# Key blocks of 114 keys instead of 128 in the attention of a decoder block

## The chip, the cores and the metric

The kernel runs on one core of a Trainium2 chip. The metric is the device time of one execution in microseconds (us), and less is better. The engines are named as in the profile: PE is TensorE's matmul and PEld its weight load, DVE is VectorE, ACT is ScalarE, POOL is GpSimd, SP is SyncE, which issues DMAs.

## The reference

One layer of a decoder: 16 learned tokens are put ahead of 1024 tokens of 1024 features (float32), then come a mixer and a gated MLP. The mixer runs a short convolution and an attention with 16 heads of 64 features side by side. Only the attention is touched here. It is a stick-breaking attention: no softmax, but a product of survival factors, taken from the query backwards.

```python
def stick_breaking_attention(q, k, v):
    # A[t,s] = sigmoid(z_ts) * prod_{s<j<t} (1 - sigmoid(z_tj)), s < t
    ...
        z = jnp.einsum("bqhd,bkhd->bhqk", qb, kb, ...) * scale
        causal = s_idx < t_idx
        log_beta = jax.nn.log_sigmoid(z)
        log_fail = jnp.where(causal, log_beta - z, 0.0)
        survive = lax.cumsum(log_fail, axis=3, reverse=True) - log_fail
        a = jnp.where(causal, jnp.exp(log_beta + survive), 0.0)
        o = jnp.einsum("bhqk,bkhd->bqhd", a, vb)
```

## The kernel before, in words

There are 1040 positions. The first 14 give no output, so 1026 queries remain: nine query blocks of `QB` = 114, in three groups `g` of three (`CH` = 342 queries). Query block `b` sees the keys from 0 to `nk` = 128 + 114 b, so the query blocks end at 128, 242, 356, 470, 584, 698, 812, 926 and 1040 keys.

Values that a product needs in more precision than one reduced-precision number gives are split into a high and a low part (`split`, lines 63 to 65: ACT copies the high part, DVE or POOL subtracts it). A dense product of the projections (`Dense.run`, lines 128 to 130, tile `mm`) is three matmuls for each block of 128 features: high by high, high by low, low by high.

Attention works through units of head pair `p`, head `h` and group `g`, in two stages that are Python generators:

- `stage1` computes the scores of a query block (`z`, lines 330 and 331), two sigmoids on ACT (`fl`, what survives, and `be`, the weight), the running product on DVE (a scan over `fl`, L340), and on POOL the weight `be` times the product (L346), a mask of the last 114 columns (`affine_select`, L348), and where the last key block that meets this query block reaches beyond `nk`, a memset of zeros up to its end (L353). `be` has queries on the partitions and keys in the columns.
- `stage2` goes over the key blocks `kb` of the group. For each it transposes the part of `be` of every query block that reaches the key block (L381, into the PSUM tile `tp`: keys on the partitions now), splits the result into `ah` and `al` (L64 on ACT, L65 on DVE), and two key blocks later multiplies: `av` += `vv[kb]` by `ah` (L371) and by `al` (L372). `vv` is the stationary operand, with the keys as contraction rows and 128 columns. A query block that doesn't reach a key block is left out on the left, so the moving operand has 342, 228 or 114 columns.

The values `vv` come from `item_v`: the features of v are transposed into blocks of keys by `tokens` (L262), nine blocks a head pair.

What sets the order of the work: the loop of lines 510 to 540 picks the next piece of `stage1` or `stage2` by the costs `COST1` and `COST2`, and after each piece puts in as many steps of the dense products (`dense.step`, three matmuls each) as the piece's share earns. So dense matmuls stand between most steps of attention on PE's queue. `stage2` yields `COST2[g] / (nkb + 3)` a piece, where `nkb` is its count of key blocks. The framework that builds the program adds the waits by the regions that instructions read and write, and has put some of the memsets ahead of work that stands before them in the code. `tp` has two PSUM buffers, `be` has six buffers and `fl` two.

Of the kernel before, what the change touches and what calls it, by code (L numbers as in the profile page):

```python
# [14 lines left out]
P = 128  # L15
# [7 lines left out]
QB = CH // 3  # L23
# [3 lines left out]
EPS = 1e-6  # L27
HALF = [(0, 258), (258, 256)]
NJ = 514


@with_exitstack
def block_kernel(ctx, tc, x, meta_tokens, g_pre_mix, w_in, channels, w_proj_conv,
                 w_proj_attn, w_out, g_post_mix, g_pre_ffn, w_up_gate, w_down,
                 g_post_ffn, out):
    nc = tc.nc

    def pool(name, bufs=1, side="left", space=None):
        kw = dict(name=name, bufs=bufs, reuse_waits="tile")
        if space is not None:  # L40
            kw["space"] = space
        else:
            kw["side"] = side
        return tc.tile_pool(**kw)
# [18 lines left out]
    def split(hi, lo, src, lo_engine=None):  # L63
        nc.scalar.copy(hi, src)  # L64
        (lo_engine or nc.vector).tensor_tensor(lo, src, hi.bitcast(F32), op=ALU.subtract)  # L65
# [93 lines left out]
    def col_block(w, c):  # L159
        return w[c]  # L160
# [84 lines left out]
    def item_v(p):  # L245
        st = {}

        def evac(ci, a, n, ps):
            if ci == 0:
                st["vt"] = work.tile([P, NT], F32, name="vt", tag="wk", bufs=4)  # L250
            vt = st["vt"]
            nc.scalar.copy(vt[:, a:a + n], ps)
            if ci < 2:
                return
            vv = heads.tile([P, 9, 2, P], F32R, name="vv", tag="vv", bufs=2)
            V[p] = vv

            def tokens(k0, kn, m):
                tp = ps_tp.tile([P, 512], F32, name="tp", tag="tp")
                for k in range(kn):  # L260
                    s0 = (k0 + k) * P
                    nc.tensor.transpose(tp[:m, k * P:(k + 1) * P], vt[:, s0:s0 + m], ident)  # L262
                tv = tp[:m, :kn * P].rearrange("p (k h d) -> p k h d", k=kn, h=2)
                split(vv[:m, k0:k0 + kn, :, 0:64], vv[:m, k0:k0 + kn, :, 64:128], tv)

            dense.defer(1, lambda: tokens(0, 4, P))
            dense.defer(2, lambda: tokens(4, 4, P))
            dense.defer(3, lambda: tokens(8, 1, 16))
        return (col_block(w_in, 40 + p), src_x, CH_K, evac)

    def items_conv(cb):
# [43 lines left out]
    def stage1(p, h, g):  # L315
        res = []
        qh, ql, kk = QH[p][h], QL[p][h], KK[p][h]
        nk_end = P + QB * (3 * g + 2)
        for b in range(3 * g, 3 * g + 3):
            nk = P + QB * b  # L320
            q0 = QB * b
            fl = work.tile([P, NT], F32, name="fl", tag="fl")[:QB]
            be = work.tile([P, NT], F32, name="be", tag="be", bufs=6)[:QB]
            nch = -(-nk // 512)
            wch = 2 * (-(-nk // (2 * nch)))
            c0 = 0
            while c0 < nk:
                n = min(wch, nk - c0)
                z = ps_z.tile([P, 512], F32, name="z", tag="z")[:QB, :n]
                nc.tensor.matmul(z, qh[:, q0:q0 + QB], kk[:, c0:c0 + n], start=True, stop=False)  # L330
                nc.tensor.matmul(z, ql[:, q0:q0 + QB], kk[:, c0:c0 + n], start=False, stop=True)  # L331
                nc.scalar.activation(fl[:, c0:c0 + n], z, AF.Sigmoid, scale=-0.125)  # L332
                nc.scalar.activation(be[:, c0:c0 + n], z, AF.Sigmoid, scale=0.125)
                c0 += n
                if late:
                    late.pop(0)()
                if c0 < nk:
                    yield n
            def weights(fl=fl, be=be, nk=nk):
                nc.vector.tensor_tensor_scan(fl[:, :nk][:, ::-1], fl[:, :nk][:, ::-1],  # L340
                                             upper[:, NT - nk:][:, ::-1], 1.0,
                                             op0=ALU.mult, op1=ALU.max)
                w = -(-(nk - 1) // (-(-nk // 384)))
                for a in range(0, nk - 1, w):
                    e = min(a + w, nk - 1)
                    nc.gpsimd.tensor_tensor(be[:, a:e], be[:, a:e], fl[:, a + 1:e + 1],  # L346
                                            op=ALU.mult)
                nc.gpsimd.affine_select(out=be[:, nk - QB:nk], in_=be[:, nk - QB:nk],  # L348
                                        pattern=[[-1, QB]], compare_op=ALU.is_gt, fill=0.0,
                                        base=0, channel_multiplier=1)  # L350
                pad = min(P * (-(-nk // P)), nk_end)
                if pad > nk:
                    nc.gpsimd.memset(be[:, nk:pad], 0.0)  # L353

            late.append(weights)
            res.append((be, nk))
            if len(res) == 3:
                units[(p, h, g)] = res
            yield n

    def stage2(p, h, g):
        blocks = units.pop((p, h, g))
        vv = V[p]
        nk_end = blocks[-1][1]
        nkb = -(-nk_end // P)
        av = ps_av.tile([P, 512], F32, name="av", tag="av")[:, :CH]
        pend = []

        def products(kb, n, off, ah, al):
            w = vv[:n, kb, h, :]  # L370
            nc.tensor.matmul(av[:, off:], w, ah[:n, off:], start=(kb == 0), stop=False)  # L371
            nc.tensor.matmul(av[:, off:], w, al[:n, off:], start=False, stop=(kb == nkb - 1))  # L372

        unit = COST2[g] / (nkb + 3)
        for kb in range(nkb):
            n = min(P, nk_end - kb * P)
            js = [j for j in range(3) if blocks[j][1] > kb * P]
            off = QB * js[0]
            tp = ps_tp.tile([P, 512], F32, name="tp", tag="tp")
            for j in js:  # L380
                nc.tensor.transpose(tp[:n, QB * j:QB * (j + 1)], blocks[j][0][:, kb * P:kb * P + n],  # L381
                                    ident[:QB, :QB])
            ah = work.tile([P, CH], F32R, name="ah", tag="ah", bufs=4)
            al = work.tile([P, CH], F32R, name="al", tag="al", bufs=4)
            split(ah[:n, off:], al[:n, off:], tp[:n, off:CH])
            pend.append((kb, n, off, ah, al))
            if len(pend) > 2:
                products(*pend.pop(0))
            yield unit
        while pend:  # L390
            products(*pend.pop(0))
            yield unit
        if (h, g) == (0, 0):
            OT[p] = work.tile([P, NT], F32, name="ot", tag="wk", bufs=4)
        ot = OT[p]
        a, b = (0, 64) if h == 0 else (64, 0)
        o = ot[a:a + 64, CH * g:CH * (g + 1)]
        nc.scalar.copy(o, av[b:b + 64])
        nc.vector.tensor_tensor(o, av[a:a + 64], o, op=ALU.add)
        if (h, g) == (1, 2):  # L400
            nc.sync.dma_start(o_d[p * P:(p + 1) * P, :], ot[:, :NQ])
        yield unit
# [17 lines left out]
    dense = Dense(ps_mm, items)  # L420
# [67 lines left out]
    def stream1():  # L488
        for u in units_in_order:
            for c in stage1(*u):  # L490
                yield c, u

    def stream2():
        for u in units_in_order:
            for c in stage2(*u):
                yield c, u
# [65 lines left out]
    k = 0  # L562
# [70 lines left out]
    k = 0  # L633
# [42 lines left out]
    early = x_ctx.enter_context(pool("early"))  # L676
    ops = {name: early.tile([P, 2, 4, NJ], F32R, name=f"op{name}") for name in ("B11", "T1")}
    par_ffn = early.tile([P, 66], F32, name="par_ffn")
# [95 lines left out]
    def op_split(name, r, which, engine):  # L774
        t = ops[name][:, :, :, r[0]:r[1]]
        split(t[:, 0], t[:, 1], quarter(r, which), engine)
# [18 lines left out]
    R0 = HALF[0]  # L795
    R1, R2 = (258, 399), (399, NJ)
    RL = (258, NJ)

# [171 lines left out]
    for b in range(9):  # L970
# [3 lines left out]
        for c in range(3):  # L974
            ps = out_products(b, c)
            if (b, c) == (8, 2):
# [4 lines left out]
                for name in ("T3", "B21", "T2"):  # L981
                    ops[name] = late.tile([P, 2, 4, NJ], F32R, name=f"op{name}")
                op_split("T2", R0, "O1", nc.vector)
# [19 lines left out]
    for k, _ in enumerate(products(0, *HALF[0], bank_of(ps_mm2, "mm"), evac_u(*HALF[0]))):  # L1003
        if k == 0:
            next(prep0)
        elif k == 1:
# [3 lines left out]
            for name in ("T4", "B22"):  # L1010
                ops[name] = late2.tile([P, 2, 4, NJ], F32R, name=f"op{name}")
        elif k == 2:
# [121 lines left out]
    for gi, fbs in enumerate(groups):  # L1134
# [14 lines left out]
        for tb in range(8):  # L1149
# [23 lines left out]
            if last:  # L1173
                a, hb, s0 = accs[tb], hbs[tb], ssqs[tb]
# [64 lines left out]
```

## Time and profile before

| | |
|---|---|
| time, median of three runs | 2033.37 us (2033.12, 2033.37, 2041.17) |
| span of the profiled execution | 2040.5 us |
| the run that the span fits | 2041.17 us, the only one longer than the span |
| PE busy | 1980.9 us, 97% of the span |
| DVE, ACT, POOL busy | 49%, 42%, 50% |
| stretch in which attention runs | about 60 to 990 us |
| mean granted clock of PE, whole span | 0.994 |

A row of a group of instructions gives line, engine and operation, output <- inputs, the shapes, the count, then busy time in us and the mean of one in ns, and behind the second bar the idle time of the engine just before them, with what ended it. In the rows of PE and PEld a shape such as `58*128 58x114` means contraction rows * columns of the stationary operand, and then the operand that is read, partitions x elements. A row of the timeline gives start and duration in us. A row of the waits says who waited for whom: total us, times, longest. A row of the stretches gives its length, the busy time of PE, PEld, DVE, ACT and POOL with their counts of instructions, the granted clock of PE, and the share and rate of DMA. Matmuls overlap, and their ends are modelled.

### The profile page before, as it was taken

How to read it: one execution, taken by the hardware profiler on the slowest of the kernel's cores; microseconds unless marked ns; L12 is line 12 of the kernel's file. 1: busy time of each engine (PE TensorE's matmuls, PEld its weight loads, DVE VectorE, ACT ScalarE, POOL GpSimd, SP SyncE). 2: the span in 40 equal slices, each digit the busy share in tenths (PEclk: the TensorE clock that was granted, in tenths of full speed). 3: DMA queues.
4: the chain of work that ended last, by engine and by line, in shares of the span. 5: the costliest groups of instructions: out<-in, count | busy, mean ns of one | idle time of the engine just before them, and what ended most of it. 6: DMA issues, size and time to landing. Idle time of an engine off the chain costs nothing.

```text
span 2040.5 us, 31024 instructions
## 1 busy us (share of the span) xinstructions
PE 1980.9 (97%) x12228; PEld 1857.9 (91%) x12228; DVE 1008.2 (49%) x1545; ACT 852.2 (42%) x1771; POOL 1025.7 (50%) x1142
## 2 busy tenths in 40 slices
PE   6999999999999999999999989979999999999997
PEld 6999999999999999999999989968998998878886
DVE  6445555555555555653331115784444434445547
ACT  5544554545454545554421213453344344421122
POOL 2644666565555646565223550246465655654353
PEclk9999999999999999999999999989999999999999
DMA  3111101111111111012574664312221212253223
GB/s 136 42 63 42 53 31 63 42 53 42 42 53 42 57 38 62 32 57 78 175 229 156 180 180 130 101 47 95 92 82 63 104 63 83 73 178 118 86 83 135
DMA packets 56175, 177.59 MB, mean 87 GB/s; under 512 B 12872, under 2 KB 12872, under 8 KB 56028
## 3 DMA queue, kind: packets, MB, share of 16 engines
q1 hardware_dynamic: 52704, 165.09, 24.7%
q10 hardware_dynamic: 3324, 10.50, 1.7%
q8 instruction: 96, 1.57, 0.3%
q14 instruction: 51, 0.42, 0.1%
HBM read 131.36 MB, written 44.21 MB: 86 GB/s over the span
## 4 chain that ended last, share of the span: by engine, by line
PE 82%; DVE 7%; DMA 5%; ACT 2%; POOL 2%; issue 1%; ACTq 0%; DVEq 0%; SPq 0%; POOLq 0%
PE mm L128 14%; PE mm L129 13%; PE mm L130 13%; PE st L867 6%; PE st L869 6%; PE st L871 6%; PE tp L381 3%; PE st L1161 3%; PE st L1159 3%; PE st L1160 3%; PE av L371 2%; PE av L372 2%; DMA xv<-in_x_dram 2%; PE z L331 2%; PE z L330 2%
## 5 line engine op out<-in xcount | busy, mean ns | idle before, releaser
L128 PE MATMUL mm<-xnT,whi 128*128 128x342 f32 (+2 forms) x1536 | 506.0, 330 | 0.3 <-ACT xnT L64 0.2
L129 PE MATMUL mm<-xnT,whi 128*128 128x342 f32 (+2 forms) x1536 | 493.5, 321 | 0.5 <-DVE xnT L65 0.5
L130 PE MATMUL mm<-xnT,wlo 128*128 128x342 f32 (+2 forms) x1536 | 492.3, 320 | 0.0
L112 POOL TENSOR_TENSOR wlo<-raw,whi 128x256 fp32r<-128x256 f32 x320 | 268.6, 872 | 203.8 <-ACT whi L109 203.1
L346 POOL TENSOR_TENSOR be<-be,fl 114x271 f32<-114x271 f32 (+14 forms) x288 | 206.0, 736 | 261.6 <-DVE fl L340 254.1
L128 PEld LDWEIGHTS mm<-xnT,whi 128*128 128x128 f32 x1536 | 289.7, 189 | 5.0 <-ACT xnT L64 0.7
L129 PEld LDWEIGHTS mm<-xnT,whi 128*128 128x128 f32 x1536 | 290.2, 189 | 2.1 <-DVE xnT L65 1.0
L130 PEld LDWEIGHTS mm<-xnT,wlo 128*128 128x128 f32 x1536 | 289.7, 189 | 0.0
L340 DVE TENSOR_TENSOR_SCAN fl<-fl,upper 114x128 f32<-114x128 f32 (+2 forms) x144 | 215.2, 1496 | 116.1 <-ACT fl L332 77.4
L65 POOL TENSOR_TENSOR a_op<-raw,a_op 128x512 fp32r<-128x512 f32 (+1 forms) x136 | 193.8, 1439 | 88.8 <-ACT a_op L64 86.6
L65 DVE TENSOR_TENSOR al<-tp,ah 128x342 fp32r<-128x342 f32 (+4 forms) x288 | 127.9, 451 | 148.7 <-ACT ah L64 146.5
L64 ACT CAST ah<-tp 128x342 fp32r<-128x342 f32 (+4 forms) x288 | 112.8, 398 | 167.2 <-PE tp L381 159.0
L867 PE MATMUL st<-opT,a_op 128*128 128x258 f32 (+2 forms) x528 | 171.2, 324 | 3.8 <-ACT snap L882 1.7
L869 PE MATMUL st<-opT,a_op 128*128 128x258 f32 (+2 forms) x528 | 169.4, 321 | 2.3 <-DVE opT L65 1.5
L871 PE MATMUL st<-opT,a_op 128*128 128x258 f32 (+2 forms) x528 | 169.1, 320 | 0.0
L332 ACT ACTIVATE fl<-z 114x348 f32<-114x348 f32 (+10 forms) x240 | 111.6, 465 | 128.2 <-PE z L331 98.6
L64 ACT CAST a_op<-raw 128x512 fp32r<-128x512 f32 (+1 forms) x136 | 85.1, 634 | 154.0 <-DMA raw<-in_w_up_gate_dram 51.1
L1166 DVE TENSOR_TENSOR acc<-acc,st 128x512 f32<-128x512 f32 x144 | 98.4, 687 | 91.1 <-PE st L1161 91.1
L869 PE MATMUL st<-opB,a_op 128*128 128x512 f32 (+2 forms) x396 | 127.5, 322 | 1.9 <-DVE opB L65 1.9
L867 PE MATMUL st<-opB,a_op 128*128 128x512 f32 (+2 forms) x396 | 127.4, 322 | 0.0
L871 PE MATMUL st<-opB,a_op 128*128 128x512 f32 (+2 forms) x396 | 127.0, 321 | 0.0
L381 PE MATMUL tp<-ident,be 114*128 114x114 f32 x720 | 118.8, 262 | 5.6 <-DVE al L65 4.5
(169 smaller groups left out, 4318.3 us busy)
## 6 DMA issues: line engine op xcount, KB each, us to landing
raw<-in_w_in_dram SPq DMA_DIRECT2D x64, 512.0 KB, 3.4
raw<-in_w_up_gate_dram SPq DMA_DIRECT2D x44, 512.0 KB, 3.3
act_d<-owork SPq DMA_DIRECT2D x22, 512.0 KB, 4.3
araw<-act_d SPq DMA_DIRECT2D x22, 512.0 KB
raw<-in_w_down_dram SPq DMA_DIRECT2D x22, 512.0 KB, 3.2
y_d<-yy SPq DMA_DIRECT2D x8, 513.0 KB
ga_d<-gt SPq DMA_DIRECT2D x8, 513.0 KB
o_d<-ot SPq DMA_DIRECT2D x8, 513.0 KB
```

The costliest lines, as they stand in the source:

```text
L64: nc.scalar.copy(hi, src)
L65: (lo_engine or nc.vector).tensor_tensor(lo, src, hi.bitcast(F32), op=ALU.subtract)
L112: nc.gpsimd.tensor_tensor(lo[:, c], raw[:, c], hi[:, c].bitcast(F32), op=ALU.subtract)
L128: nc.tensor.matmul(ps, wh, xh, start=(kb == 0), stop=False)
L129: nc.tensor.matmul(ps, wh, xl, start=False, stop=False)
L130: nc.tensor.matmul(ps, wl, xh, start=False, stop=(kb == KB - 1))
L340: nc.vector.tensor_tensor_scan(fl[:, :nk][:, ::-1], fl[:, :nk][:, ::-1], upper[:, NT - nk:][:, ::-1], 1.0, op0=ALU.mult, op1=ALU.max)
L346: nc.gpsimd.tensor_tensor(be[:, a:e], be[:, a:e], fl[:, a + 1:e + 1], op=ALU.mult)
L381: nc.tensor.transpose(tp[:n, QB * j:QB * (j + 1)], blocks[j][0][:, kb * P:kb * P + n], ident[:QB, :QB])
L867: nc.tensor.matmul(ps, wt[:, 0, k], xh, start=start and kb == 0, stop=False, skip_group_check=True)
L869: nc.tensor.matmul(ps, wt[:, 0, k], xl, start=False, stop=False, skip_group_check=True)
L871: nc.tensor.matmul(ps, wt[:, 1, k], xh, start=False, stop=stop and kb == 3, skip_group_check=True)
```

## The change

The key blocks end where the query blocks end. There is one of 128 keys and there are eight of 114; before there were eight of 128 keys and one of 16. Groups of 356, 698 and 1040 keys took blocks of 128 with a last one of 100, 58 and 16 keys; now every block but the first has 114. The counts of key blocks stay 3, 6 and 9. No query block ends inside a key block now, so the memsets go.

```diff
+KEYS = [(0, P)] + [(P + QB * i, QB) for i in range(8)]
...
             def tokens(k0, kn, m):
...
-                    s0 = (k0 + k) * P
+                    s0 = KEYS[k0 + k][0]
...
-            dense.defer(3, lambda: tokens(8, 1, 16))
+            dense.defer(3, lambda: tokens(8, 1, QB))
...
     def stage1(p, h, g):
-        nk_end = P + QB * (3 * g + 2)
...
-                pad = min(P * (-(-nk // P)), nk_end)
-                if pad > nk:
-                    nc.gpsimd.memset(be[:, nk:pad], 0.0)
...
     def stage2(p, h, g):
-        nk_end = blocks[-1][1]
-        nkb = -(-nk_end // P)
+        nkb = 3 * g + 3
...
         for kb in range(nkb):
-            n = min(P, nk_end - kb * P)
-            js = [j for j in range(3) if blocks[j][1] > kb * P]
+            k0, n = KEYS[kb]
+            js = [j for j in range(3) if blocks[j][1] > k0]
...
-                nc.tensor.transpose(tp[:n, QB * j:QB * (j + 1)], blocks[j][0][:, kb * P:kb * P + n],
+                nc.tensor.transpose(tp[:n, QB * j:QB * (j + 1)], blocks[j][0][:, k0:k0 + n],
                                     ident[:QB, :QB])
```

On PE, the end of the first unit of the second group, before: the last key block's transpose, and further on its two products (`av`, 114 columns), with dense matmuls (`mm`) between. The shape is that of the output; the contraction rows of a product are the keys of its key block, 58 here.

```order
L381 MATMUL tp<-ident,be 58x114
L371 MATMUL av<-ah,vv 128x342
L372 MATMUL av<-al,vv 128x342
L128 MATMUL mm<-xnT,whi 128x342
L129 MATMUL mm<-xnT,whi 128x342
L130 MATMUL mm<-xnT,wlo 128x342
```

The same place now:

```order
L377 MATMUL tp<-ident,be 114x114
L367 MATMUL av<-ah,vv 128x342
L368 MATMUL av<-al,vv 128x342
L129 MATMUL mm<-xnT,whi 128x342
L130 MATMUL mm<-xnT,whi 128x342
L131 MATMUL mm<-xnT,wlo 128x342
```

Nothing has moved: the instruction stands at the same place of PE's queue and writes 114 keys instead of 58, and the line numbers differ by the added and removed lines.

On POOL, a later unit of the second and third group, before: the memsets of `be`, the weight multiplications (L346), the masks, and the low halves of dense weights (`wlo`, L112), with what each waits for.

```order
L112 TENSOR_TENSOR wlo<-raw,whi 128x256 x3
L353 MEMSET be 114x84 [waits PE_49]
L346 TENSOR_TENSOR be<-be,fl 114x349 [waits DVE_49]
L346 TENSOR_TENSOR be<-be,fl 114x348 [waits Activation_49]
L353 MEMSET be 114x98 [waits PE_49]
L348 AFFINE_SELECT be<-be 114x114 [waits Pool_49]
L346 TENSOR_TENSOR be<-be,fl 114x271 [waits DVE_49]
```

The same place now:

```order
L113 TENSOR_TENSOR wlo<-raw,whi 128x256 x3
L346 TENSOR_TENSOR be<-be,fl 114x349 [waits DVE_49]
L346 TENSOR_TENSOR be<-be,fl 114x348 [waits Activation_49]
L348 AFFINE_SELECT be<-be 114x114 [waits Pool_49]
L346 TENSOR_TENSOR be<-be,fl 114x271 [waits DVE_49,PE_49]
```

The two memsets are gone, and the first multiplication of the next query block waits for PE beside DVE.

## The prediction

> **What bounds the kernel now.** First the profile's first page, for the engine that is full; then the stretches of the program, for where the change lies.
>
> ```profile
> span 2040.5 us, 31024 instructions
> ...
> PE 1980.9 (97%) x12228; PEld 1857.9 (91%) x12228; DVE 1008.2 (49%) x1545; ACT 852.2 (42%) x1771; POOL 1025.7 (50%) x1142
> ...
> 60.00:990.00 930.00, 923.02 (x6035) 892.84 (x6035) 483.86 (x696) 471.50 (x1075) 522.02 (x757) 1.00 0.15 50
> ```
>
> The last row is the stretch from 60 to 990 us, where attention is mixed with the dense products: PE busy 923 of 930 us at a granted clock of 1.00, DVE and ACT about half, POOL 522. So in this stretch only the number and the spacing of PE's instructions count, and everything that the change touches lies in it. A busy PE hides one thing: matmuls overlap, so a matmul of 0.32 us may cost 0.16. What a matmul costs is the distance from its start to the next start, and I read that from the timeline.
>
> **PE's work, by form.** The counts first. Before, a head's three query groups need 3, 6 and 9 key blocks of 128, and after 3, 6 and 9 blocks of which the first has 128 keys and the others 114; the query blocks that each key block meets are the same (3, then 2, then 1 in the last two). The instructions of every engine keep number and order; only POOL loses 80. What changes on PE is the shape, and the shapes that matter are the last key blocks of the groups, which hold 100, 58 and 16 keys now and 114 then. The groups of matmuls and weight loads, kept apart by form (contraction rows * columns of the stationary operand, then the moving one):
>
> ```profile
> L381 PE MATMUL tp<-ident,be 114*128 114x114 f32 x672 | 105.8, 262 | 3.5 <-DVE al L65 2.6 <-DVE vv L65 0.2
> ...
> L371 PE MATMUL av<-ah,vv 58*128 58x114 f32 x16 | 5.1, 318 | 0.0
> L371 PE MATMUL av<-ah,vv 16*128 16x114 f32 x16 | 5.1, 317 | 0.0
> ...
> L381 PE MATMUL tp<-ident,be 114*16 114x114 f32 x16 | 4.2, 262 | 0.0
> ...
> L371 PE MATMUL av<-ah,vv 100*128 100x114 f32 x16 | 3.6, 225 | 0.0
> ...
> L371 PEld LDWEIGHTS av<-ah,vv 100*128 100x128 f32 x16 | 3.0, 189 | 0.0
> ...
> L371 PEld LDWEIGHTS av<-ah,vv 58*128 58x128 f32 x16 | 2.9, 183 | 3.4 <-issue 3.4
> L371 PEld LDWEIGHTS av<-ah,vv 16*128 16x128 f32 x16 | 2.9, 181 | 3.4 <-issue 3.2 <-ACT gt L303 0.2
> ```
>
> The three rows of L371 have the same moving size, 114 columns, and differ in contraction rows alone. With 100 rows the matmul takes 225 ns; with 58 or 16 it takes 318 or 317, and its weight load stands idle 3.4 us in sixteen cases, 0.21 us each, for nothing that the profile can name. The timeline shows the places (PE first, then the weight loads, then PE again for 100 and for 16 rows):
>
> ```profile
> 346.67 0.32 PE L130 MATMUL mm<-xnT,wlo 128*128 128x342 f32 x1
> 346.92 0.32 PE L371 MATMUL av<-ah,vv 58*128 58x114 f32 x1
> ...
> 347.27 0.42 PE L128 MATMUL mm<-xnT,whi 128*128 128x342 f32 x1
> 347.54 0.32 PE L129 MATMUL mm<-xnT,whi 128*128 128x342 f32 x1
> ...
> 346.91 0.18 PEld L371 LDWEIGHTS av<-ah,vv 58*128 58x128 f32 x1 [0.22 <-issue]
> ...
> 83.12 0.33 PE L130 MATMUL mm<-xnT,wlo 128*128 128x344 f32 x1
> 83.28 0.22 PE L371 MATMUL av<-ah,vv 100*128 100x114 f32 x1
> ...
> 83.45 0.38 PE L128 MATMUL mm<-xnT,whi 128*128 128x344 f32 x1
> 83.66 0.32 PE L129 MATMUL mm<-xnT,whi 128*128 128x344 f32 x1
> ...
> 83.12 0.19 PEld L371 LDWEIGHTS av<-ah,vv 100*128 100x128 f32 x1
> ...
> 424.47 0.32 PE L130 MATMUL mm<-xnT,wlo 128*128 128x342 f32 x1
> 424.72 0.32 PE L371 MATMUL av<-ah,vv 16*128 16x114 f32 x1
> ...
> 425.33 0.32 PE L129 MATMUL mm<-xnT,whi 128*128 128x342 f32 x1
> ```
>
> From the start of the dense matmul ahead to the start of the second one behind: 347.54 - 346.67 = 0.87 us with 58 rows, 425.33 - 424.47 = 0.86 with 16, and 83.66 - 83.12 = 0.54 with 100. The same four matmuls stand in each stretch. With 100 rows the weights are loaded from 83.12, while the matmul ahead still runs; with 58 they are loaded at 346.91, a hundredth before their matmul, and the delay comes again on the way back to 128 rows.
>
> **The change, part by part.**
>
> 1. *The last key blocks of the second and third query group.* 16 heads by 2 groups make 32 tails, of 58 and 16 rows now and 114 then. No row shows a product of this kind with 114 rows. The nearest is 100 rows, which costs nothing extra; 128 rows lies on its other side. I take 114 as 100: 32 x (0.865 - 0.54) = 10.4 us, and from 9.8 to 11.0 by the hundredths to which the starts are given. All of it lies on PE, with the dense matmuls behind it waiting for nothing else, so it comes off the span.
>
> 2. *The other products* go from 128 to 114 rows (from 100 in the first group's tail). By the rows of 100 and 128 they keep their spacing: 0.
>
> 3. *The transposes* load 114 columns instead of 128 in 576 cases less 48 tails, and 114 instead of 100, 58 or 16 in the tails. Their moving operand stays the identity, 114 wide, and the duration is 262 ns with 128 and with 16 columns: 0. How far they stand apart shows a row of three:
>
> ```profile
> 340.61 0.46 PE L381 MATMUL tp<-ident,be 114*128 114x114 f32 x3
> ```
>
> 0.46 us less the 0.26 of the last leaves two spacings of 0.10. If these went with the loaded columns, 14 of 128 of 0.10 us in the 432 places where a transpose follows another would be a gain of 4.8 us, which is the bound on that side; on the other side see the last rival.
>
> 4. *ACT and DVE* split tiles of 114 instead of 128 partitions with the same columns; they are half idle, and I take 0. One transpose of v per head pair (16 columns before, 114 after) with its split is also of the same moving size: 0.
>
> 5. *80 memsets go from POOL*, and their waits with them.
>
> ```profile
> L353 POOL MEMSET be<- x80: 103/145/182, 69.8 to 942.8; 114x14 f32 x16, 114x42 f32 x16, 114x56 f32 x16, 114x84 f32 x16
> ...
> POOL be L353 <- PE tp L381: 63.5, 36, 5.8
> ...
> ACT fl L332 <- POOL be L353: 9.4, 8, 2.6
> ...
> 403.90 0.11 POOL L353 MEMSET be<- 114x14 f32 x1 [1.75 <-PE tp L381]
> 409.90 0.41 POOL L346 TENSOR_TENSOR be<-be,fl 114x127 f32<-114x127 f32 x1 [5.89 <-DVE fl L340]
> ```
>
> Busy 80 x 0.145 = 11.6 us and waiting 63.5 us, on an engine that goes on to wait for DVE: the memset at 403.90 has waited 1.75 us for PE, and POOL then stands 5.89 us until the scan of L340 is done. No PE wait in this stretch names these memsets. ACT's 9.4 us behind them could reach PE through the scores; nothing to 3 us, and I take 0. Seventy multiplications of L346 carry a wait for PE afterwards that they did not have; they write columns that ACT has written just before, which it may do only once PE has read the old content, so these waits end earlier than ACT's and cost 0. What is queued behind them on POOL are weight halves (L112).
>
> The sum: 10.4 us. The span of 2040.5 us belongs to the run of 2041.17, the only one of the three that is longer than it, with 0.7 us around it; there I expect 2030.8. The median run, 2033.37, is 7.8 us shorter; what differs lies outside the stretch above, which has its full clock, so the term stays: 2033.4 - 10.4 = 2023.0.
>
> A rule to weigh against the rows of L371. The Trainium skill, page "TensorE: Matmul & The Clock Gate", section "LDWEIGHTS (loading the stationary operand)", says that a load's time goes with its columns and not with the contraction rows. The durations (189, 183, 181 ns) agree with it; the spacing does not, and by the rule alone the sum would be 0. The Trainium skill, page "TensorEngine Tiling (Array Packing)", section "Key Properties", says that changing the tiling mode drains the TensorE; if loads of up to 64 rows and of more are two modes, the 0.87 against 0.54 agrees, and the sum stays 10.4.
>
> **The rivals.**
>
> *No change that can be told: other engines give the gain back.* PE waits in this stretch almost only for the splits of transposed weights:
>
> ```profile
> PEld tp L381 <- DVE al L65: 9.9, 18, 2.4
> ...
> PE tp L381 <- DVE al L65: 4.5, 8, 2.1
> ...
> 372.99 0.17 PE z L331
> ...
> 373.19 0.40 ACT fl L332
> ...
> 373.76 1.93 DVE fl L340
> 375.69 0.42 DVE al L65
> ```
>
> These 26 waits could grow by what PE gains ahead of them. Against it: the chain that ended last runs there from a score matmul (L331) over the sigmoid and the scan to the split, so it begins on PE and shifts with it. If 10 of the 32 tails were lost that way, 3.3 us come back: 2026.3. Also here: that the delay of the 58-row matmul is how it is recorded, and no cost; the start of the dense matmuls behind it speaks against that. Then 2033.
>
> *A gain of more.* The bound of part 3 and ACT's waits of part 5: 2033.4 - 10.4 - 4.8 = 2018.2.
>
> *Slower: 114 rows are treated like 58.* The products then lose their early load in every key block but the first. 15 such blocks a head, 2 of them tails that are slow already: 16 x 13 x 0.33 = 69 us, 2102. It decides at whether the loads of 114 rows show the idle 0.21 us. For it: no row of this product has 114. Against it: 100 rows, further from 128, are not delayed, and the transposes, which contract over 114 rows, take 0.10 us each.
>
> *Slower by the columns.* Loads of fewer than 128 columns could be of a slower kind. If each of the 528 transposes that load 114 instead of 128 stood 0.10 us further apart (its spacing doubled), it would be 53 us, 2086. The loads of the transposes by columns:
>
> ```profile
> L381 PEld LDWEIGHTS tp<-ident,be 114*128 114x128 f32 x672 | 84.8, 141 | 11.8 <-DVE al L65 5.7 <-DVE vv L65 1.7
> ...
> L381 PEld LDWEIGHTS tp<-ident,be 114*100 114x100 f32 x16 | 2.0, 126 | 4.5 <-DVE al L65 4.3
> L381 PEld LDWEIGHTS tp<-ident,be 114*58 114x58 f32 x16 | 1.7, 108 | 0.0
> ```
>
> They go nearly in a line, 15 ns for 28 columns and 18 for 42, with no step below 128. The Trainium skill, page "TensorE: Matmul & The Clock Gate", section "Weight-path perf modes — Fast Weight Load (FWL) and DoubleRow", has a fast load that needs 128 weights and an input type other than FP32; these rows, of a type it leaves out, agree with it.
>
> **How the numbers follow.** A measurement of this kernel tells about 0.5%, 10.2 us, from no change; the forecast of 10.4 us lies just beyond it, so the main case falls on both sides. Chances: the main case (2021 to 2025) 0.62, of which 0.40 faster by over 0.5% and 0.22 within; a gain of more 0.14, all faster; given back or no cost at all 0.20, all within; the two slower ones 0.04. Faster 0.54, same 0.42, slower 0.04. The time is that of the main case, 2023. The range runs from the bound of the larger gain, 2018, to 2031: the upper end takes in a partial loss and a median that falls on a run like that of 2041.17 (2030.8). The main case has its own range of 2021 to 2025.
>
> **What would show it.** In the profile after: the rows of this product with 114 rows and 114 columns have a mean near 225 ns and a load without idle time (part 1); the stretch from the dense matmul ahead of a tail to the second behind is 0.54 us in all three groups; the transposes stay at 262 ns (part 3); no memset of `be`, and POOL's wait for PE is gone with PE's own waits unchanged (part 5). It is wrong if loads of 114 rows show idle time, or if the waits of the transposes for DVE grow by several us.

## The result, and the profile after

The changed kernel takes 2020.39 us (median of six runs, 2019.35 to 2021.89) beside 2035.38 us (2032.43 to 2041.17) before. The ratio is 0.9925, with a 95% interval from 0.9908 to 0.9942: 15.0 us less, and by the interval 12 to 19. The forecast was 2023.0, with a range of 2018 to 2031. The profiled execution has a span of 2018.2 us and took 2019.99. A second set of five runs (experiment 4) gave 2017.67 beside 2031.08, ratio 0.9933 (0.9920 to 0.9946), 13.4 us less.

The first page and the stretch with attention, which now ends at about 980 us:

```profile
span 2018.2 us, 30990 instructions
...
PE 1968.4 (98%) x12228; PEld 1857.0 (92%) x12228; DVE 1006.3 (50%) x1545; ACT 853.3 (42%) x1771; POOL 1022.7 (51%) x1062
...
60.00:980.00 920.00, 914.55 (x6050) 894.85 (x6050) 483.64 (x698) 473.14 (x1079) 519.19 (x677) 1.00 0.15 51
```

PE has the same 12228 instructions and POOL 80 fewer. The groups of the products, the transposes and the transposed v by form (L367, L377 and L263 were L371, L381 and L262):

```profile
L377 PE MATMUL tp<-ident,be 114*114 114x114 f32 x576 | 96.5, 262 | 4.0 <-DVE al L66 3.4
...
L367 PE MATMUL av<-ah,vv 114*128 114x114 f32 x48 | 10.6, 220 | 0.0
L263 PE MATMUL tp<-ident,vt 128*114 128x128 f32 x8 | 2.6, 323 | 0.0
...
L377 PEld LDWEIGHTS tp<-ident,be 114*114 114x114 f32 x576 | 71.1, 134 | 13.7 <-DVE al L66 8.8 <-issue 0.3
L367 PEld LDWEIGHTS av<-ah,vv 114*128 114x128 f32 x240 | 45.3, 189 | 0.7
```

The 48 products of 114 columns have one form now and a mean of 220 ns, where it was 318, 317 and 225. The 3.4 us of unexplained idle time ahead of each of the two short forms are gone: 0.7 us is left over all 240 loads. The timeline at a tail of the second group, the same one that the prediction shows at 346.67:

```profile
343.70 0.32 PE L131 MATMUL mm<-xnT,wlo 128*128 128x342 f32 x1
343.86 0.22 PE L367 MATMUL av<-ah,vv 114*128 114x114 f32 x1
343.91 0.27 PE L368 MATMUL av<-al,vv 114*128 114x114 f32 x1
344.02 0.38 PE L129 MATMUL mm<-xnT,whi 128*128 128x342 f32 x1
344.24 0.32 PE L130 MATMUL mm<-xnT,whi 128*128 128x342 f32 x1
```

344.24 - 343.70 is 0.54 us, where it was 0.87.

PE's matmuls stand in the same order in both kernels, so the distance from each start to the next can be compared one by one. Over the 32 tails (the last products of the second and third query group, with the dense matmuls around them) the mean of the four distances together is 0.867 us before and 0.539 after. In the stretch of attention (the matmuls that start between 55 and 985 us in the profile of before) the sums are, in us (the second profiles are those of e4_before and e6_after, experiments 3 and 4):

| distances | before | before, second profile | after | after, second profile |
|---|---|---|---|---|
| the four at each of the 32 tails | 27.75 | 27.74 | 17.25 | 17.25 |
| into the first transpose of a key block | 54.72 | 54.18 | 52.98 | 53.17 |
| transpose to transpose | 43.55 | 43.50 | 43.26 | 43.47 |
| into, between and out of the transposes of v | 10.87 | 10.85 | 11.25 | 11.26 |
| all others | 793.26 | 793.35 | 793.21 | 794.53 |
| sum | 930.14 | 929.63 | 917.95 | 919.68 |

The tails give 10.50 and 10.49 us in the two pairs of profiles. Attention as a whole gives 12.2 and 9.9 us; a third pair, the kernels of experiment 5, which are these two up to 1000 us, gives 929.08 - 920.27 = 8.8. Profiles of one kernel differ here too. The second profile after spends 7.9 us on the matmuls around 105 us where the first spends 6.3; from 104 to 108 us its granted clock is 0.64, and 1.00 in the first. (In that job e5 and e7 have this slow place too, and e8, the kernel before with early loads, does not; whether the change has a part in it stays open.) Most of the rest lies in the waits into the transposes (experiment 3).

The first two profiles differ by 22.3 us in span; 8.5 us of it lie around 1200 us, in the last projection, where the change touches nothing (experiments 4 and 5).

### The profile page after: what moved, and what is told of

It reads as the page before. It is cut to its first block, busy times and chain, and to the rows that moved or that the text cites. A ratio compares the mean times of both kernels' runs of the same rounds, so it can differ in the third digit from the quotient of the medians.

```text
span 2018.2 us, 30990 instructions
## 1 busy us (share of the span) xinstructions
PE 1968.4 (98%) x12228; PEld 1857.0 (92%) x12228; DVE 1006.3 (50%) x1545; ACT 853.3 (42%) x1771; POOL 1022.7 (51%) x1062
## 3 DMA queue, kind: packets, MB, share of 16 engines
q10 hardware_dynamic: 3324, 10.50, 1.7%
## 4 chain that ended last, share of the span: by engine, by line
PE 87%; DVE 7%; ACT 2%; DMA 2%; POOL 1%; issue 1%; ACTq 0%; DVEq 0%; SPq 0%; POOLq 0%
PE mm L129 14%; PE mm L130 14%; PE mm L131 14%; PE st L863 7%; PE st L867 7%; PE st L865 7%; PE tp L377 3%; PE st L1157 3%; PE st L1155 3%; PE st L1156 3%; PE av L368 2%; PE av L367 2%; PE z L331 2%; PE z L330 2%; PE po L706 1%; PE po L708 1%
## 5 line engine op out<-in xcount | busy, mean ns | idle before, releaser
L346 POOL TENSOR_TENSOR be<-be,fl 114x271 f32<-114x271 f32 (+14 forms) x288 | 206.0, 736 | 310.3 <-DVE fl L340 301.6
L113 POOL TENSOR_TENSOR wlo<-raw,whi 128x256 fp32r<-128x256 f32 x320 | 254.8, 828 | 208.2 <-ACT whi L110 207.3
L340 DVE TENSOR_TENSOR_SCAN fl<-fl,upper 114x128 f32<-114x128 f32 (+2 forms) x144 | 214.4, 1490 | 112.2 <-ACT fl L332 64.0
L66 DVE TENSOR_TENSOR al<-tp,ah 114x342 fp32r<-114x342 f32 (+3 forms) x288 | 128.3, 452 | 148.8 <-ACT ah L65 147.5
L65 ACT CAST ah<-tp 114x342 fp32r<-114x342 f32 (+3 forms) x288 | 113.0, 398 | 165.3 <-PE tp L377 157.0
L377 PE MATMUL tp<-ident,be 114*114 114x114 f32 (+1 forms) x720 | 118.5, 262 | 4.1 <-DVE al L66 3.4
```

The lines of the kernel that those rows point to most:

```text
L113: nc.gpsimd.tensor_tensor(lo[:, c], raw[:, c], hi[:, c].bitcast(F32), op=ALU.subtract)
```

## The experiments

The runs were made in jobs, and the level of the kernel before differs from job to job (2035, 2041, 2031 us, and 2042 in a single run), so times are compared within a job, or as ratios. Expected times that start from 2020.4 stand at the level of the first job.

**1. How many contraction rows it takes.** The tails of the changed kernel with fewer rows: 64 (e1_rows64) or 65 (e2_rows65) of the 114. The other 50 or 49 keys are left out of the sum.

```diff
-            w = vv[:n, kb, h, :]
-            nc.tensor.matmul(av[:, off:], w, ah[:n, off:], ...)
-            nc.tensor.matmul(av[:, off:], w, al[:n, off:], ...)
+            m1, m2 = (64, 64) if g > 0 and kb == nkb - 1 else (n, n)      # e2_rows65: (65, 65)
+            nc.tensor.matmul(av[:, off:], vv[:m1, kb, h, :], ah[:m1, off:], ...)
+            nc.tensor.matmul(av[:, off:], vv[:m2, kb, h, :], al[:m2, off:], ...)
```

> The changed kernel, but the two products of the last key block in the second and third query group (32 tails) contract over the first 64 of the 114 keys only; the other 50 keys are left out of the sum. Instructions, order and all other shapes stay. Theory (a contraction over at most 64 rows is not covered by the matmul ahead): each tail costs 0.33 us again, 32 x 0.33 = 10.4 us over the changed kernel's 2020.4, so about 2031, with 0.21 us idle before the weight load of these products, and no more than 2035 if the waits for DVE come back too. Rival (the gain comes from the missing memsets and from where the waits fall, not from the rows): no more than 2 us over 2020.4.

> The same with the first 65 of the 114 keys in the 32 tails; the other 49 are left out. Theory with a step between 64 and 65 rows: as the changed kernel, 2020.4, within 1 us, and 0.54 us a tail. Rival (the cost grows as rows go missing, between the 58 and the 100 rows of the kernel before): about four fifths of 10.4 us, 2028 to 2029.

Measured: 64 rows 2040.53 us, ratio to before 0.9991 (0.9983 to 1.0000), so the gain is all but gone; 65 rows 2029.98 us, ratio 0.9941 (0.9927 to 0.9954), so it is there. One row is worth 10.55 us between the medians. The groups, 64 rows and then 65:

```profile
L367 PE MATMUL av<-ah,vv 64*128 64x114 f32 x32 | 10.2, 318 | 0.0
...
L367 PEld LDWEIGHTS av<-ah,vv 64*128 64x128 f32 x32 | 5.8, 183 | 6.8 <-issue 6.5 <-ACT gt L304 0.2
```

```profile
L367 PE MATMUL av<-ah,vv 65*128 65x114 f32 x32 | 7.0, 218 | 0.0
...
L367 PEld LDWEIGHTS av<-ah,vv 65*128 65x128 f32 x32 | 6.0, 188 | 0.0
```

With 64 rows the matmul is at 318 ns again and its load idles 6.8 us in 32 cases; with 65 there is nothing of it. The tails take 0.867 and 0.539 us. It is a step between 64 and 65 rows and not a slope. And the kernel e1 has every other part of the change, the missing memsets among them, and is only 0.9 us from the kernel before (0.0 to 3.5 by the interval), so the tails carry nearly all of the gain.

**2. What is paid for: the load or the way in and out.** First one of the two products short (e5_one64), then four products in a row, short (e9_short4) or of full height (e10_full4). In e5 the low part of 50 keys is left out of the sum; e9 counts 64 keys of the last block twice and leaves out 50, and e10 counts the whole block twice.

```diff
 # e5_one64
+            m1, m2 = (n, 64) if g > 0 and kb == nkb - 1 else (n, n)
 # e9_short4; e10_full4 has m = n
+            tail = g > 0 and kb == nkb - 1
+            m = 64 if tail else n
+            w, two = vv[:m, kb, h, :], (0, 1) if tail else (0,)
+            for r in two:
+                nc.tensor.matmul(av[:, off:], w, ah[:m, off:], ...)
+                nc.tensor.matmul(av[:, off:], w, al[:m, off:], ...)
```

> The changed kernel, but only the second product of each of the 32 tails (low part, L372 of the kernel before) contracts over 64 of the 114 keys; the low part of the other 50 is left out. Theory (each load of at most 64 rows, and the one that follows it, is not covered by the matmul ahead): 0.10 us before the second product, 0.09 behind it and 0.05 one further, 32 x 0.24 = 7.5 us over the changed kernel. Rival (the cost is paid at each switch between short and full height, two a tail as with both products short): the full 10.4 us over it.

> The changed kernel, but the 32 tails contract over 64 of the 114 keys and issue their two products twice in a row (the last key block counts twice, and 50 of its keys not at all), so that four short products stand in a row. Theory (each load of at most 64 rows is uncovered): every distance from one short product to the next is 0.157 us. Rival (the cost belongs to the switch between heights): the distances in the middle fall to the 0.056 us of full-height products of 114 columns, and only the way in and out is long.

> The same with all 114 keys, so four full-height products in a row: the measure beside which the short ones stand. Both theories: 0.05 to 0.11 us from one to the next, set by the covered load or the 114 columns.

One short product: 2027.59 us, 9.9 over the changed kernel in the same job (2017.67), between the 7.5 and the 10.4 that were expected. At the tails it costs 0.815 - 0.539 = 0.276 us, 8.8 us over 32. So neither expectation held, and the second short product adds only 0.05. The two kernels with four in a row ran once each, 2046.34 us short and 2037.68 full, beside 2042.39 for the kernel before; what follows rests on the distances in their profiles. Short and then full:

```profile
112.09 0.32 PE L131 MATMUL mm<-xnT,wlo 128*128 128x342 f32 x1
112.34 0.32 PE L370 MATMUL av<-ah,vv 64*128 64x114 f32 x1
112.50 0.27 PE L371 MATMUL av<-al,vv 64*128 64x114 f32 x1
112.61 0.28 PE L370 MATMUL av<-ah,vv 64*128 64x114 f32 x1
112.72 0.27 PE L371 MATMUL av<-al,vv 64*128 64x114 f32 x1
112.93 0.43 PE L129 MATMUL mm<-xnT,whi 128*128 128x342 f32 x1
113.19 0.32 PE L130 MATMUL mm<-xnT,whi 128*128 128x342 f32 x1
```

```profile
111.76 0.32 PE L131 MATMUL mm<-xnT,wlo 128*128 128x342 f32 x1
111.92 0.22 PE L370 MATMUL av<-ah,vv 114*128 114x114 f32 x1
111.98 0.28 PE L371 MATMUL av<-al,vv 114*128 114x114 f32 x1
112.09 0.27 PE L370 MATMUL av<-ah,vv 114*128 114x114 f32 x1
112.20 0.27 PE L371 MATMUL av<-al,vv 114*128 114x114 f32 x1
112.31 0.38 PE L129 MATMUL mm<-xnT,whi 128*128 128x342 f32 x1
112.53 0.32 PE L130 MATMUL mm<-xnT,whi 128*128 128x342 f32 x1
```

The distances, medians over 32 tails, in ns from the dense matmul ahead: short 248, 157, 112, 112, 201, 261; full 158, 55, 110, 112, 112, 216. In the middle of the row short products follow each other as fast as full ones, at 112 ns. (The 0.056 us that the rival expected there stand, with full height too, only between the first product and the second.) And only the first load of each row stands idle: in e9 it is 6.8 us over all 64 loads of `ah`, as over the 32 of e1, and nothing over those of `al`:

```profile
L371 PEld LDWEIGHTS av<-al,vv 64*128 64x128 f32 x64 | 12.0, 187 | 0.0
L370 PEld LDWEIGHTS av<-ah,vv 64*128 64x128 f32 x64 | 11.9, 185 | 6.8 <-issue 6.6 <-ACT gt L304 0.2
```

The difference is 1091 - 763 = 328 ns, the same as with two short products (0.867 - 0.539). So from two short products to four the cost does not grow: it belongs to the way from full height to at most 64 rows and back, once for each visit. The theory that each short load is uncovered falls. The Trainium skill, page "TensorEngine Tiling (Array Packing)", section "Key Properties", has the rule that changing the tiling mode drains the TensorE. If a product of at most 64 contraction rows is in another mode than one of full height, which that section does not say, these rows agree, with the first short matmul 0.25 us behind the dense one instead of 0.16. What the rule does not tell is why the second distance is long as well (157 ns), and why one short product costs 0.276 and two or four cost 0.328; no run here separates that.

**3. The memsets, and the kernel before once more.**

```diff
 # e3_memsets: the changed kernel with
+                pad = min(P * (-(-nk // P)), P + QB * (3 * g + 2))
+                if pad > nk:
+                    nc.gpsimd.memset(be[:, nk:pad], 0.0)
```

> The changed kernel with the 80 memsets put back, on the columns on which they stood before; nobody reads these columns now. Theory (POOL is off the path): 2020.4 within 1 us, POOL 11.6 us busier and waiting for PE again. Rival (the 1.9 us that attention gained beyond the tails come from POOL's freedom): 1.5 to 3 us longer, and the scans of 584 columns at the start of a head pair at 1.97 us instead of 1.37.

> The kernel before, unchanged, for a second profile and more times. Theory (the 8.5 us around 1200 us of the first profile, a DMA wait of 5.8 us and a half clock after it, belong to some runs only): times spread from 2032 to 2041, and a profile without that wait is about 2032 to 2034. Rival (the change took them away): the wait is there in nearly all runs, and the median lies at 2036 or above.

The kernel with the memsets took 2030.05 us, ratio 0.9944 (0.9929 to 0.9958), and e2, without them and in the same job but with 65 rows at the tails, 2029.98, so they cost nothing that can be told. POOL waits as before, by this row of e3's waits:

```profile
POOL be L353 <- PE tp L380: 63.7, 36, 5.8
```

Its attention takes 919.14 us by the sums of the table, between the two profiles of the changed kernel (917.95 and 919.68).

The waits into the transposes go with something else. The scan of 584 columns on DVE (L340) runs 16 times, and in every profile some of the 16 take 1.90 to 1.98 us and the others 1.37 to 1.50. Counted over ten profiles, beside the distances into the first transpose of a key block:

| slow scans of 16 | us into the first transpose | profiles |
|---|---|---|
| 2 | 52.98, 53.00, 53.17 | after, e2, e6 |
| 3 | 53.52 to 53.73 | e1, e3, e5, e7, e8 |
| 4 | 54.18 | e4 |
| 5 | 54.72 | before |

So a slow scan goes with half a microsecond of waiting. The kernels with memsets (before, e3, e4, e8) have 3 to 5 slow scans and those without 2 or 3; e3 and e8 have as many as e1, e5 and e7. Which scans are slow differs between two profiles of the same kernel. A share of the memsets in this is not shown.

The kernel before beside itself: ratio 0.9997 (0.9989 to 1.0006), median 2041.97, times from 2037 to 2045. Its second profile has the wait near 1200 us as well. That is what the rival expected, but the kernels with the change in this job, e2 and e3, have the wait too.

**4. The changed kernel again.** Nothing is edited in e6_after.

> The changed kernel again, unchanged, beside the kernel before, for a second profile and more times. Theory (the change is worth the 32 tails, 10.5 us, and 1 to 2 us of waits of the transposes; the rest of the 15.0 us between the first medians is a DMA wait and a clock halved around 1200 us that fell more often on the runs of before): 11 to 13 us shorter than before on this chip, a ratio of 0.994 to 0.9945. Rival (the change takes that wait away too): a ratio near 0.9925, and a profile without a wait of several us there.

The ratio of 0.9933 (0.9920 to 0.9946) lies between the two expectations, and its interval holds one end of each. The profiles say more. From 1150 to 1240 us, before, after, and the second profile after (e6); the row of each is preceded here by PE's wait, where there is one:

```profile
PE mm L128 <- DVE gal L619: 6.2, 2, 5.8
...
1150.00:1240.00 90.00, 83.44 (x512) 82.59 (x512) 18.93 (x45) 19.87 (x41) 42.88 (x44) 0.96 0.66 180
```

```profile
PE mm L129 <- DVE gal L615: 1.3, 1, 1.3
...
1150.00:1240.00 90.00, 88.67 (x572) 88.35 (x571) 31.22 (x78) 26.32 (x60) 35.38 (x36) 1.00 0.63 179
```

```profile
1150.00:1240.00 90.00, 90.00 (x583) 89.96 (x581) 32.97 (x80) 26.34 (x60) 35.39 (x36) 1.00 0.60 178
```

Before, PE waits 5.8 us for a DVE product whose input arrives late, and then has a clock of 0.96 over these 90 us; after, it waits 1.3 us or not at all, at full clock. But the kernel with 65 rows, which has the same gain in attention, has the wait too:

```profile
PE mm L129 <- DVE gal L615: 6.7, 2, 6.4
...
1150.00:1240.00 90.00, 83.25 (x521) 82.38 (x520) 27.13 (x65) 23.44 (x52) 35.27 (x36) 0.96 0.60 171
```

So the wait does not go with the rows. Of the kernels with the gain, e2, e3 and e7 show it in their profiles, and the two profiles of the changed kernel don't. It looks more like a matter of the job: the four profiles of one job (e1 to e4) all have a longest wait of 5.9 to 6.6 us there, whatever the kernel, and of the four of the other (e5 to e8) only e7 has one.

**5. That wait, attacked at its loads.** The inputs `gal` and `ml` of the last projection are asked for earlier, in both kernels.

```diff
             if ci == 0:
-                st["g"] = sw.tile(...); st["m"] = sw.tile(...)
-                nc.sync.dma_start(st["g"][:, :NQ], ga_d[...])
-                nc.sync.dma_start(st["m"][:, :NQ], m_d[...])
+                load_g(ob); load_mm(ob)                    # where not loaded yet
+                st["g"], st["m"] = pa_in["g", ob], pa_in["m", ob]
+                load_mm(ob + 1)
+            if ci == 1:
+                load_g(ob + 1)
```

> The changed kernel with the gates and the convolution branch of the next block of 128 features (tiles gal and ml, 513 KB each) asked for one chunk or more earlier in the last projection. Theory (the wait of 1 to 7 us around 1200 us is for these loads, late behind weight loads): the wait goes, and with it the halved clock behind it; up to 8 us shorter than the changed kernel, and the spread of times narrower. Rival (DMA is full there, and what is asked for earlier only pushes other loads back): no gain, the wait moves to another load.

> The kernel before with the same earlier loads. Theory: as much shorter than the kernel before as the earlier loads make the changed kernel shorter, so that the two with early loads differ by the 11 to 13 us of the change. Rival (the change and the wait hang together): the difference between the two is far from that.

The changed kernel with early loads took 2026.22 us, 8.5 longer than without in the same job, and the kernel before with them 2030.80, ratio 0.9996 (0.9987 to 1.0005). The wait in the changed kernel is back at 5.5 us:

```profile
PE mm L129 <- DVE gal L629: 5.5, 1, 5.5
```

The theory that these loads only have to be asked for earlier is wrong; the rival, that DMA is full there and another load is pushed back, fits but was not shown. The difference between the two kernels with early loads is 4.6 us, far from that of the change. But e8's profile does not have the wait (1.4 us at most), so the two differ in it:

```profile
PEld mm L128 <- DVE gal L633: 1.4, 1, 1.4
```

The profiles of e8 and e6 are one of each kernel without the wait, though e8 has the early loads: their spans differ by 11.3 us, of which attention has 9.4. So 8 us in this stretch come and go, in kernels that are the same up to 1000 us. DVE waits for the load of `gal` there in all ten profiles, 4.7 to 6.7 us at the longest; what decides whether PE has to wait as well stays open.

## Why the prediction was right, point by point

- *What bounds the kernel.* Right for attention: the gain lies in distances on PE, and POOL's 80 memsets with 63.5 us of waiting moved nothing that can be told.
- *Part 1, the tails.* Forecast 10.4 us, measured 10.50, and by the mechanism that was named; 114 rows behave as 100, and as 65. The rival in which 114 rows are treated like 58 is excluded: 0.7 us idle over 240 loads.
- *Part 2, the other products.* No cost: the other distances sum to 793.3 us before and 793.2 after. The 794.5 of the second profile after has the slow clock near 105 us in it.
- *Part 3, the transposes.* 262 ns with 114 columns as with 128. Where one follows another the sum fell by 0.3 and 0.03 us in the two pairs, against a bound that the prediction gives as 4.8. The last rival (a slower load) is excluded too: 134 ns with 114 columns, on the line between 126 and 141.
- *Part 4.* The transpose of v with 114 columns was taken as 0. It went from 277 to 323 ns, 8 times, and the sum of that kind rose by 0.4 us, nearly all of it in the distance to the next matmul behind these eight. A small miss.
- *Part 5 and the rival that gives the gain back.* The waits into the transposes were expected to stay. They fell: PE's from 9.9 and 4.5 us to these rows of after,

```profile
PEld tp L377 <- DVE al L66: 8.8, 17, 2.4
...
PE tp L377 <- DVE al L66: 3.4, 5, 2.1
```

  and the distances into the transposes by 1.7 and 1.0 us in the two pairs, but by only 0.1 between e8 and e7. In the first pair the gain lies at six places with 0.25 to 0.31 us each; at one of them a scan of 584 columns on DVE ran 1.97 us before and 1.37 after, with the same POOL subtractions (`wlo`, L112, now L113) beside it:

```profile
709.75 1.97 DVE L340 TENSOR_TENSOR_SCAN fl<-fl,upper 114x584 f32<-114x584 f32 x1
```

```profile
701.70 1.37 DVE L340 TENSOR_TENSOR_SCAN fl<-fl,upper 114x584 f32<-114x584 f32 x1
```

  In the second profile of the changed kernel the scan at this place runs 1.97 us again (at 701.25), and in the kernel before the scan at 371.63 runs 1.37. So this term is as much how a profile fell as the change. Why a scan is long or short was not tested.
- *The sum.* Attention gave 8.8 to 12.2 us where 10.4 stood, and 10.3 as the mean of three profiles each (929.6 and 919.3). The medians differ by 15.0 and 13.4 us. The rest, some 3 to 5 us, is what the sum did not have: it took the stretch around 1200 us as the same in both, and there the first two profiles differ by 8.5 us. That the rest lies there in the runs that have no profile is not shown. The median of before was itself taken from three runs as 2033.4 and is 2035.4 with six.
- *The chances.* The case that came is the main one with its time just outside its own range (2020.4 against 2021 to 2025), on the side of faster by over 0.5%. That the wide range still held it is in part luck: its lower end came from part 3, a gain that did not come, and not from anything around 1200 us.

## What to carry to other kernels

When a loop over blocks leaves a short last block on the contraction side of a matmul, look at the distances from start to start around it, not at the durations alone: here two or four products of 64 rows or fewer (16, 58 and 64 were measured) between matmuls of full height cost 0.33 us for each visit, and 65 rows cost nothing. Cut the blocks evenly, so that no contraction falls to 64 rows or fewer, if the number of blocks stays the same; if short products are unavoidable, put them together, since four in a row paid no more than two. And a difference between two profiles should be laid out along the program before it is credited to a change: here a stretch that the change does not touch held over a third of it, and a second profile of the same kernel showed what else comes and goes.

## What the runs showed of the hardware that was not expected

- The step between 64 and 65 contraction rows is sharp: 318 against 218 ns for the first matmul of a tail, 0.867 against 0.539 us for the tail.
- The cost is one of switching: distances of 112 ns inside a run of short products, equal to full height, with 0.33 us for the way in and out, and 0.28 if only one product is short.
- A DVE scan of the same 584 columns takes 1.37 to 1.50 us or 1.90 to 1.98, at different places in two profiles of one kernel, and a slow one goes with about half a microsecond of waiting on PE.
